# Two-layer hybrid trunk: the state-space outputs stand one position further behind their within-chunk kernels

## The chip, the cores and the metric

The kernel runs on 1 core of one Trainium2 chip. The metric is the device time of one execution in microseconds (us). Three executions of the kernel before took 2449.69, 2453.62 and 2454.12 us (median 2453.62). A fourth, with the profiler on, took 2454.61 us; its profile has a span of 2452.6 us from the first to the last instruction. All engine times below are from that one.

## The reference, cut to what matters

A batch of one, 256 tokens of width 2048, two layers. Each layer is a mixer with two branches side by side (stick-breaking attention, and an S5 diagonal state-space branch), merged by gates, then a channel mixer (dense SwiGLU in layer 0, top 2 of 8 experts in layer 1). The part that is touched is the state-space branch:

```python
def hybrid_mixer(h, w_in, ...):
    q, k, v, u, gate_a, gate_b = jnp.split(h @ w_in, cuts, axis=-1)
    o_attn = stick_breaking_attention(heads(q), heads(k), heads(v))
    y = jax.nn.gelu(s5_ssm(u, a_re, a_im, log_dt, b_re, b_im, c_re, c_im, d_skip))
    o_ssm = y * jax.nn.sigmoid(y @ w_glu)
    merged = (jax.nn.sigmoid(gate_a) * (o_attn @ p_attn)
              + jax.nn.sigmoid(gate_b) * (o_ssm @ p_ssm))
    return merged @ w_out

def s5_ssm(u, ...):                       # 64 groups of 16 channels, 64 complex states each
    ...
    _, _, x_re, x_im = lax.associative_scan(combine, (a_re_t, a_im_t, bu_re, bu_im), axis=1)
    y = einsum('bsgn,gpn->bsgp', x_re, c_re) - einsum('bsgn,gpn->bsgp', x_im, c_im) + d_skip * u
```

## The kernel before, in words

**The foreground.** Almost all the work is dense products of 256 token rows (two blocks of 128) with float32 weights. `chunk_mm` (L151) does 512 output columns at a time: it loads weights in tiles `wr` of two slices of 128 rows (512 KB) on the SP queue, splits each into a rounded part `wh` (ScalarE, L145) and a remainder `wl` (VectorE, L148), and issues three matmuls per slice and block (L166, L167, L168), each 128x512. Four slices make 24 matmuls; then it calls `pump()`. The pools `wr`, `wh` and `wl` have four buffers each, so the split runs at most four tiles, or 48 matmuls, ahead of TensorE.

**The background.** `pump()` advances Python generators, each by its rate, in steps that end at a `yield`. That decides where the small instructions of the attention heads and of the state-space branch stand between groups of 24 foreground matmuls, on every engine; after it, a scheduler may still shift single instructions. Each engine then works its own list in order: an instruction that waits holds everything behind it on that engine. The state-space generator runs at 1.05 steps per pump (`R_SSM`), and from the outputs on it is the only one left in the background, or nearly.

**The state-space branch.** The 256 steps are cut in 32 chunks of 8. For each of 8 blocks of 8 groups (index `gg`) `ssm_out` does:

- `products` (VectorE, L511 to L513, into the tile `PA`, with a ScalarE copy at L690): C times powers of A.
- `kern(gg)`: 8 matmuls (L635) give the response within a chunk; ScalarE copies it out of PSUM into `K2` (L639), VectorE adds the skip term (L642), the POOL queue writes it to a scratch in DRAM with 4 DMAs (L644, `kscr<-K`) and reads it back in Toeplitz form with one DMA of 512 KB (L651, `T<-kscr`). That read waits for the four writes.
- `outp(gg)`: 16 matmuls (L658 with `T`, L661 with `PA` and the chunk states `XS`), then a gelu on ScalarE (L665).
- `turn(gg)`: two transposes (L673) and a VectorE copy (L678). After the blocks 3 and 7 the POOL queue writes four blocks to DRAM (L681); both halves are read back as `yt` (L877) and copied on ScalarE (L880) where the gated output needs them.

A loop over `t` (L685) holds these in a software pipeline: in one turn of the loop `turn(t-3)`, the products of `t`, a yield, `outp(t-2)`, `kern(t-1)`, a yield. `outp` is held back until the attention is done. `PA`, `ptmp`, `K2`, `T` and `Y` all come from one pool of 28 slabs of 4 KB per partition, which the gates and the activations share: a slab can be written again only when its last reader is done.

The foreground around it is: the attention's output product (`oh` matmuls, 8 slices, 48 matmuls) and gate projections (`hh`, 16 slices, 96 matmuls), in turn.

Of the kernel before, what the change touches and what calls it, by code (L numbers as in the profile page):

```python
# [51 lines left out]
class Trunk:  # L52
# [558 lines left out]
    def ssm_out(self, l, U2, yscr):  # L611
        nc, i = self.nc, self.i
        V = nc.vector
        sp = self.sp

        dI = self.small([16, 16], tag="dI", bufs=1)
        self.tc.keep_in_program_order(nc.gpsimd.memset(dI, 0.0))
        for j in range(4):
            nc.gpsimd.dma_start(
                dI[j * 32 : j * 32 + 16],  # L620
                i["ssm_d"][l].rearrange("(a j) c -> j a c", j=4)[j].partition_broadcast(16))
        V.tensor_tensor(dI, dI, self.i16.unsqueeze(1).to_broadcast([P, 16, 16]), op=OP.mult)
        PA, T, Y = {}, {}, {}

        def wide(g):

            return sp["bA"][:, g : g + 2].rearrange("n g p -> n (g p)")

        def kern(gg):

            K2 = self.slab([8, 2, 16], name="K2")
            ps = self.paux()
            for gl in range(8):
                j, q = gl % 4, gl // 4
                nc.tensor.matmul(  # L635
                    ps[j * 32 : (j + 1) * 32, q * P : (q + 1) * P],
                    wide(gg * 8 + gl),
                    PA[gg][:, gl].rearrange("p t c -> p (t c)"), start=True, stop=True)
            nc.scalar.copy(  # L639
                K2.rearrange("p t q c -> p q t c"),  # L640
                ps[:, 0:256].rearrange("p (q t c) -> p q t c", q=2, t=8))
            V.tensor_tensor(K2[:, 0], K2[:, 0], dI[:, gg * 2 : gg * 2 + 2], op=OP.add)  # L642
            for j in range(4):
                nc.gpsimd.dma_start(  # L644
                    self.kscr[gg][:, 7:15, j * 32 : (j + 1) * 32],
                    K2[j * 32 : j * 32 + 16].rearrange("p t q c -> p t (q c)"))

            T[gg] = self.slab([8, 8, 16], name="T")
            ks = self.kscr[gg]
            win = bass.AP(ks.tensor, ks.offset, [[15 * P, 16], [P, 8], [1, 8 * P]])  # L650
            nc.gpsimd.dma_start(T[gg].rearrange("p t g c -> p (t g c)"), win)  # L651

        def outp(gg):
            ps = self.paux()
            for gl in range(8):
                j, q = gl % 4, gl // 4
                o = ps[j * 32 : (j + 1) * 32, q * P : (q + 1) * P]
                nc.tensor.matmul(  # L658
                    o.rearrange("c (t p) -> c t p", t=8), U2[gg // 4][:, gl, gg % 4], T[gg][:, :, j * 2 + q],
                    start=True, stop=False)  # L660
                nc.tensor.matmul(  # L661
                    o, self.XS[:, :, 0, gg * 8 + gl], PA[gg][:, gl].rearrange("p t c -> p (t c)"),
                    start=False, stop=True)
            yc = self.small([2, 16, 8], tag="sy", bufs=2)
            nc.scalar.activation(  # L665
                yc.rearrange("p q c t -> p q t c"),
                ps[:, 0:256].rearrange("p (q t c) -> p q t c", q=2, t=8), AF.Gelu_apprx_tanh)
            return yc

        def turn(gg, yc):  # L670
            ps = self.paux()
            for q in range(2):
                nc.tensor.transpose(  # L673
                    ps[:, q * P : (q + 1) * P], yc[:, q].rearrange("p c t -> p (c t)"), self.ident)
            h = gg // 4
            if gg % 4 == 0:
                Y[h] = self.slab([8, 4, 32], name="ysb")
            nc.vector.tensor_copy(Y[h][:, :, gg % 4], ps[:, 0:256].rearrange("p (g c) -> p g c", g=8))  # L678
            if gg % 4 == 3:

                nc.gpsimd.dma_start(  # L681
                    yscr[h].rearrange("(g q) j n -> (q j) g n", g=8), Y[h].rearrange("p g a c -> p g (a c)"))

        YC = {}
        for t in range(11):  # L685
            if t > 2:
                turn(t - 3, YC.pop(t - 3))
            if t < 8:
                PA[t] = self.slab([8, 8, 16], name="PA")
                nc.scalar.copy(PA[t][:, :, 0], sp["cA"][:, t * 8 : t * 8 + 8])  # L690

                self.products(t, PA[t][:, :, 1:8], sp["cA"], sp["cB"], 0, 7)
            yield
            if 2 <= t < 10:
                while not self.attn_done:
                    yield
                YC[t - 2] = outp(t - 2)
            if 1 <= t < 9:
                kern(t - 1)
            yield  # L700
# [610 lines left out]
```

## Time and profile before

| | |
|---|---|
| Median of three executions | 2453.62 us (2449.69 to 2454.12) |
| The profiled execution | 2454.61 us, span 2452.6 us |
| TensorE (PE) busy | 2395.9 us, 98% of the span |
| VectorE, ScalarE busy | 1630.7 us (66%), 1358.3 us (55%) |
| POOL busy | 100.6 us (4%) |
| State-space outputs, layer 0 and layer 1 | about 308 to 434 us and 1436 to 1556 us of the span |

PE is the TensorE matmul row, PEld its weight loads, DVE is VectorE, ACT is ScalarE, SP the queue that loads weights. A matmul's duration overlaps with the next one's, so the pace of PE is read from the starts of successive instructions and not from their durations. The profile puts a wait down to what released it.

### The profile page before, as it was taken

How to read it: one execution, taken by the hardware profiler on the slowest of the kernel's cores; microseconds unless marked ns; L12 is line 12 of the kernel's file. 1: busy time of each engine (PE TensorE's matmuls, PEld its weight loads, DVE VectorE, ACT ScalarE, POOL GpSimd, SP SyncE). 2: the span in 40 equal slices, each digit the busy share in tenths (PEclk: the TensorE clock that was granted, in tenths of full speed). 3: DMA queues.
4: the chain of work that ended last, by engine and by line, in shares of the span. 5: the costliest groups of instructions: out<-in, count | busy, mean ns of one | idle time of the engine just before them, and what ended most of it. 6: DMA issues, size and time to landing. Idle time of an engine off the chain costs nothing. (4 is left out here: it accounts for less than half of the span.)

```text
span 2452.6 us, 31712 instructions
## 1 busy us (share of the span) xinstructions
PE 2395.9 (98%) x11813; PEld 1959.6 (80%) x11813; DVE 1630.7 (66%) x1930; ACT 1358.3 (55%) x1676; POOL 100.6 (4%) x180
## 2 busy tenths in 40 slices
PE   9999988999999999999999999999999999999997
PEld 7878867888888888888888787788878888888875
DVE  7576954465545454454676866446558898988987
ACT  6455543544544444444546554454447777777775
POOL 0101011000000000000010011000000000000000
PEclk9999999999999999999999999999999999999998
DMA  7865466665556656566785556666549899898995
GB/s 262 227 193 172 151 197 178 214 215 184 185 192 187 190 190 187 190 205 199 224 275 157 155 172 208 196 194 208 175 143 362 309 346 360 294 357 312 367 360 192
DMA packets 297954, 556.99 MB, mean 227 GB/s; under 512 B 35552, under 2 KB 36896, under 8 KB 297792
## 3 DMA queue, kind: packets, MB, share of 16 engines
q1 hardware_dynamic: 284944, 517.52, 64.0%
q0 software_dynamic: 12848, 37.37, 5.1%
q8 instruction: 94, 1.54, 0.3%
q14 instruction: 68, 0.56, 0.1%
HBM read 543.86 MB, written 10.94 MB: 226 GB/s over the span
## 5 line engine op out<-in xcount | busy, mean ns | idle before, releaser
L148 DVE TENSOR_TENSOR wl<-wr,wh 128x1024 fp32r<-128x1024 f32 (+1 forms) x764 | 928.2, 1223 | 663.8 <-ACT wh L145 657.5
L145 ACT CAST wh<-wr 128x1024 fp32r<-128x1024 f32 (+1 forms) x764 | 801.6, 1053 | 851.3 <-PE pm L168 782.4
L166 PE MATMUL pm<-wh,hh 128*128 128x512 f32 x1536 | 605.6, 394 | 0.5 <-ACT hh L193 0.3
L167 PE MATMUL pm<-wl,hh 128*128 128x512 f32 x1536 | 600.9, 391 | 3.4 <-DVE wl L148 3.4
L168 PE MATMUL pm<-wh,hl 128*128 128x512 f32 x1536 | 600.5, 391 | 0.3 <-DVE hl L194 0.3
L167 PEld LDWEIGHTS pm<-wl,hh 128*128 128x128 f32 x1536 | 289.2, 188 | 64.1 <-DVE wl L148 6.2
L166 PEld LDWEIGHTS pm<-wh,hh 128*128 128x128 f32 x1536 | 289.0, 188 | 61.9 <-issue 1.2
L168 PEld LDWEIGHTS pm<-wh,hl 128*128 128x128 f32 x1536 | 289.1, 188 | 60.8 <-DVE hl L194 0.9
L148 DVE TENSOR_TENSOR wl<-ring,wh 128x1024 fp32r<-128x1024 f32 x214 | 254.9, 1221 | 22.3 <-ACT wh L145 15.9
L145 ACT CAST wh<-ring 128x1024 fp32r<-128x1024 f32 x214 | 221.7, 1053 | 50.6 <-PE pm L168 47.8
L167 PE MATMUL pm<-wl,eh 128*128 128x512 f32 x512 | 202.3, 395 | 1.3 <-DVE wl L148 0.8
L166 PE MATMUL pm<-wh,eh 128*128 128x512 f32 x512 | 200.5, 392 | 1.4 <-ACT wh L145 1.4
L168 PE MATMUL pm<-wh,el 128*128 128x512 f32 x512 | 201.1, 393 | 0.0
L167 PE MATMUL pm<-wl,ah 128*128 128x512 f32 x512 | 200.2, 391 | 0.2 <-DVE wl L148 0.2
L168 PE MATMUL pm<-wh,al 128*128 128x512 f32 x512 | 199.9, 390 | 0.0
L166 PE MATMUL pm<-wh,ah 128*128 128x512 f32 x512 | 199.7, 390 | 0.0
L167 PEld LDWEIGHTS pm<-wl,eh 128*128 128x128 f32 x512 | 96.5, 188 | 28.6 <-DVE wl L148 8.8
L166 PEld LDWEIGHTS pm<-wh,eh 128*128 128x128 f32 x512 | 96.5, 188 | 21.5 <-ACT wh L145 1.5
L167 PEld LDWEIGHTS pm<-wl,ah 128*128 128x128 f32 x512 | 96.2, 188 | 21.2 <-DVE wl L148 1.5
L166 PEld LDWEIGHTS pm<-wh,ah 128*128 128x128 f32 x512 | 96.2, 188 | 19.8
L168 PEld LDWEIGHTS pm<-wh,el 128*128 128x128 f32 x512 | 96.6, 189 | 19.2
L168 PEld LDWEIGHTS pm<-wh,al 128*128 128x128 f32 x512 | 96.2, 188 | 19.6
(310 smaller groups left out, 2566.9 us busy)
## 6 DMA issues: line engine op xcount, KB each, us to landing
wr<-in_w_in_dram SPq DMA_DIRECT2D x254, 512.0 KB, 3.9
ring<-in_moe_w_up_dram SPq DMA_DIRECT2D x72, 512.0 KB, 5.8
ring<-in_moe_w_gate_dram SPq DMA_DIRECT2D x71, 512.0 KB, 5.9
ring<-in_moe_w_down_dram SPq DMA_DIRECT2D x71, 512.0 KB, 5.9
wr<-in_w_out_dram SPq DMA_DIRECT2D x64, 512.0 KB, 3.8
wr<-in_ffn_w_gate_dram SPq DMA_DIRECT2D x64, 512.0 KB, 4.2
wr<-in_ffn_w_up_dram SPq DMA_DIRECT2D x64, 512.0 KB, 3.5
wr<-in_ffn_w_down_dram SPq DMA_DIRECT2D x64, 512.0 KB, 3.9
```

The lines of the kernel that those rows point to most:

```text
L145: t = self.nc.scalar.copy(h, raw)
L148: self.nc.vector.tensor_tensor(l, raw, h, op=OP.subtract)
L166: nc.tensor.matmul(ps[b], XH(k, b), h, start=st, stop=False)
L167: nc.tensor.matmul(ps[b], XH(k, b), l, start=False, stop=False)
L168: nc.tensor.matmul(ps[b], XL(k, b), h, start=False, stop=sp)
```

## The change

The loop over `t` has one turn more (12 for 11); `outp` and `turn` move one turn later, `kern` and the products stay. So one more `T` and one more `PA` are alive at a time, and the last output and its transposes stand later in the foreground.

```diff
-        for t in range(11):
-            if t > 2:
-                turn(t - 3, YC.pop(t - 3))
+        for t in range(12):
+            if t > 3:
+                turn(t - 4, YC.pop(t - 4))
             if t < 8:
                 PA[t] = self.slab([8, 8, 16], name="PA")
...
             yield
-            if 2 <= t < 10:
+            if 3 <= t < 11:
                 while not self.attn_done:
                     yield
-                YC[t - 2] = outp(t - 2)
+                YC[t - 3] = outp(t - 3)
             if 1 <= t < 9:
                 kern(t - 1)
```

On TensorE, layer 0, the end of the first attention output product. Before, the last two of the 16 matmuls of `outp(0)` stand here, and `kern(1)` and the gate projection follow (`pa` is a PSUM tile of the background, `pm` of the foreground):

```order
L658 MATMUL pa_2990<-T_2905,U_97_502 32x128
L661 MATMUL pa_2990<-PA_2769,XS_1108 32x128
L635 MATMUL pa_3010<-PA_2847,bA_957 32x128 x8
L166 MATMUL pm_3030<-wh_3034,hh_116 128x512
L167 MATMUL pm_3030<-wl_3035,hh_116 128x512
L168 MATMUL pm_3030<-wh_3034,hl_120 128x512
```

Now only `kern(1)` stands at that place:

```order
L167 MATMUL pm_2911<-wl_2963,oh_1998 128x512
L168 MATMUL pm_2911<-wh_2962,ol_1999 128x512
L635 MATMUL pa_2991<-PA_2847,bA_957 32x128 x8
L166 MATMUL pm_3011<-wh_3015,hh_116 128x512
L167 MATMUL pm_3011<-wl_3016,hh_116 128x512
L168 MATMUL pm_3011<-wh_3015,hl_120 128x512
```

and `outp(0)`, with the same `T_2905`, comes 48 foreground matmuls later, ahead of `kern(2)`:

```order
L658 MATMUL pa_3091<-T_2905,U_97_502 32x128
L661 MATMUL pa_3091<-PA_2769,XS_1108 32x128
L635 MATMUL pa_3111<-PA_2948,bA_957 32x128 x8
L166 MATMUL pm_3011<-wh_3130,hh_118 128x512
L167 MATMUL pm_3011<-wl_3131,hh_118 128x512
```

Counted over both layers, 40 to 48 foreground matmuls stood between a `kern(gg)` and its `outp(gg)` (72 for the first of layer 1); now 96 stand there, and 72 in four cases: blocks 2 and 3 of layer 0, blocks 6 and 7 of layer 1. The last `turn` stands 48 foreground matmuls later in layer 0 and 24 in layer 1. The numbers of instructions are the same on every engine.

On ScalarE, the copy into `PA` for block 6 of layer 0, with the semaphores that each instruction waits for (DMASW are the POOL queue's DMAs, DMAHW the weight loads). Before:

```order
L639 COPY K_676_3341<-pa_3342 128x2x8x16 [waits DMASW5_49,DMASW6_49,DMASW0_49,DMASW7_49,DVE_49,PE_49]
L145 CAST wh_3492<-wr_3490 128x1024 [waits DMAHW6_49,PE_49]
L145 CAST wh_3538<-wr_3536 128x1024 [waits DMAHW7_49,DVE_49,PE_49]
L690 COPY PA_3400<-cA_2705 128x8x16
L145 CAST wh_3544<-wr_3542 128x1024 [waits DMAHW0_49,DVE_49,PE_49]
```

Now:

```order
L639 COPY K_673_3318<-pa_3319 128x2x8x16 [waits PE_49]
L856 ACTIVATE ga_3258<-ga_3258 128x1024 [waits Activation_49]
L145 CAST wh_3462<-wr_3460 128x1024 [waits DMAHW5_49,DVE_49,PE_49]
L145 CAST wh_3468<-wr_3466 128x1024 [waits DMAHW6_49,DVE_49,PE_49]
L690 COPY PA_3376<-cA_2705 128x8x16 [waits DMASW4_49,DMASW3_49,DMASW5_49,DMASW2_49,DVE_49]
L145 CAST wh_3514<-wr_3512 128x1024 [waits DMAHW7_49,PE_49]
L145 CAST wh_3520<-wr_3518 128x1024 [waits DMAHW0_49,PE_49]
```

With more slabs alive, the slab of this `PA` is the one that `K2` has just left: the copy waits for the four DMAs that write `K_673` to DRAM, and the casts of weights stand behind it. Five of the 16 `PA` copies wait so now (two of layer 0, three of layer 1) that did not before.

## Rows read from the trace of the kernel before

**Rows 1.** The page: busy us, share of the span and instructions of each engine.
```profile
PE 2395.9 (98%) x11813; PEld 1959.6 (80%) x11813; DVE 1630.7 (66%) x1930; ACT 1358.3 (55%) x1676; POOL 100.6 (4%) x180
```
**Rows 2.** Waits of PE: waiting line, releaser, us in total, times, longest.
```profile
PE pa L658 <- DMA T<-kscr: 25.7, 12, 4.9
PE pm L167 <- DVE wl L148: 4.3, 7, 1.8
```
**Rows 3.** Stretches: length, busy us (instructions) by engine, PEclk, DMA share, GB/s.
```profile
308.00:434.00 126.00, 110.40 (x795) 88.44 (x794) 67.72 (x74) 51.61 (x65) 23.16 (x44) 0.96 0.62 185
434.00:1436.00 1002.00, 999.72 (x4685) 822.89 (x4684) 577.83 (x684) 483.84 (x606) 25.51 (x42) 1.00 0.62 196
1436.00:1556.00 120.00, 109.50 (x791) 88.58 (x790) 67.51 (x73) 54.88 (x68) 21.62 (x41) 0.97 0.62 187
```
**Rows 4.** PE in order of time: start, duration, instruction, [idle before, releaser].
```profile
308.31 0.65 PE L635 MATMUL pa<-PA,bA 128*32 128x128 f32 x16
...
317.89 0.39 PE L166 MATMUL pm<-wh,oh 128*128 128x512 f32 x1
...
319.71 0.39 PE L168 MATMUL pm<-wh,ol 128*128 128x512 f32 x1
324.17 0.45 PE L658 MATMUL pa<-T,U 128*32 128x128 f32 x8 [4.08 <-DMA T<-kscr]
...
1519.51 0.46 PE L658 MATMUL pa<-T,U 128*32 128x128 f32 x8 [0.67 <-DMA T<-kscr]
...
1520.39 0.69 PE L635 MATMUL pa<-PA,bA 128*32 128x128 f32 x16
1521.02 0.50 PE L166 MATMUL pm<-wh,hh 128*128 128x512 f32 x1
...
1535.80 0.68 PE L658 MATMUL pa<-T,U 128*32 128x128 f32 x8 [4.95 <-DMA T<-kscr]
```
**Rows 5.** Stretches behind the four longest of these waits; columns as above.
```profile
324.10:328.50 4.40, 4.33 (x54) 3.53 (x55) 1.33 (x2) 1.01 (x2) 1.27 (x3) 0.61 0.06 18
382.00:386.20 4.20, 4.20 (x54) 3.33 (x53) 0.19 (x1) 1.83 (x3) 1.52 (x3) 0.63 0.25 92
411.00:414.00 3.00, 2.92 (x49) 2.53 (x50) 0.00 (x0) 0.68 (x2) 0.00 (x0) 0.54 0.56 187
1535.70:1541.40 5.70, 5.60 (x58) 4.69 (x59) 0.19 (x1) 1.20 (x3) 1.83 (x4) 0.61 0.07 21
```
**Rows 6.** POOL in order of time, block 0 of layer 0.
```profile
312.63 2.09 POOL L644 DMA_DIRECT2D kscr<-K  x4 [97.85 <-DVE K L642]
318.23 0.53 POOL L651 DMA_DIRECT2D T<-kscr  x1 [3.51 <-DMA kscr<-K]
```
**Rows 7.** Tile T: instruction times in ns (min/median/max), and DMA landing.
```profile
L651 POOL DMA_DIRECT2D T<-kscr x16: 533/536/547, 318.2 to 1543.4; - x16
...
DMA to landing us min/median/max: 4.2/5.9/7.5
```
**Rows 8.** Tile K: the same.
```profile
L644 POOL DMA_DIRECT2D kscr<-K x64: 528/531/542, 312.6 to 1541.1; - x64
...
DMA to landing us min/median/max: 1.7/2.9/6.4
```
**Rows 9.** Groups by line: busy us, mean ns of one, idle before.
```profile
L148 DVE TENSOR_TENSOR wl<-wr,wh 128x1024 fp32r<-128x1024 f32 (+1 forms) x764 | 928.2, 1223 | 663.8 <-ACT wh L145 657.5
L145 ACT CAST wh<-wr 128x1024 fp32r<-128x1024 f32 (+1 forms) x764 | 801.6, 1053 | 851.3 <-PE pm L168 782.4 <-DMA wr<-in_w_in_dram 38.9 <-issue 16.9
L511 DVE TENSOR_TENSOR PA<-cA,AT 128x896 f32<-128x896 f32 x16 | 17.3, 1083 | 0.0
```
**Rows 10.** Tiles yscr and yt in layer 0: POOL's writes and reads, ACT's copies.
```profile
L681 POOL DMA_DIRECT2D yscr<-ysb x2: 909/910/912, 372.5 to 433.0; - x2
L877 POOL DMA_DIRECT2D yt<-yscr x2: 554/561/568, 433.9 to 437.9; - x2
L880 ACT COPY yf<-yt x2: 2079/2083/2087, 468.6 to 474.1; 128x1024 f32<-128x1024 f32 x2
...
DMA to landing us min/median/max: 4.7/4.8/4.8
```

## The prediction

> **What bounds the kernel now.** I read the busy shares first: PE is busy for 98% of the span, the next engine for 66% [rows 1]. What PE doesn't do while others work is therefore lost time, and what others wait for costs nothing. Next the waits of PE: by far the largest is L658, the first matmul of `outp`, which waits for the DMA that reads `T`: 25.7 us in 12 of 16 cases, at most 4.9 us; the second is 4.3 us [rows 2]. Then the busy times by stretch: in the 1002 us between the two state-space stretches PE is busy for 999.7 us at a granted clock of 1.00; in the two stretches for 110.4 of 126 us and 109.5 of 120 us, at 0.96 and 0.97 [rows 3]. So these 246 us have two losses: the waits, and a lower clock. The order of PE in time shows the first and the stretches behind the long waits the second: after a wait of 4.08 us PE runs at 0.61 for some 4 us, and so behind the one of 4.95 us and two more [rows 4, 5]; a clock of 0.61 is a mixture of the two levels, 1.2 and 2.4 GHz.
>
> Why `T` is late: block 0 of layer 0 starts `kern` at 308.31 us, POOL issues the four writes at 312.63 and the read at 318.23 when the writes have landed, and PE goes on at 324.17 [rows 4, 6]. The chain takes 15.9 us. Block 6 of layer 1 takes 15.4 us (1520.39 to 1535.80) [rows 4]. In that time PE has 40 to 48 foreground matmuls to do. Eight of them take 1.82 us (317.89 to 319.71), so 0.2275 us each and 10.9 us for 48 [rows 4].
>
> **What the change removes.** With 96 foreground matmuls between `kern` and its `outp` the cover is 21.8 us, plus the `outp` and `kern` of neighbouring blocks that stand between (1519.51 to 1521.02, 1.5 us) [rows 4]. In the four cases with 72 it is 16.4 + 1.5 = 17.9 us, and 17.3 us for the last block of layer 1, which has only an `outp` between (0.9 us). The longest chain of the trace that ended in a wait, 15.9 us, is below each of these. All 12 waits should go: 25.7 us.
>
> The lower clock goes with them, since it stands behind the four longest of them. What it costs is the missing share of the clock times the stretch [rows 5]: 0.39 x 4.4 = 1.72, 0.37 x 4.2 = 1.55, 0.46 x 3.0 = 1.38, 0.39 x 5.7 = 2.22; sum 6.9 us. As a check: 0.04 x 126 + 0.03 x 120 = 8.6 us by the whole stretches, which holds the time at low clock inside the waits as well [rows 3]. I take 6.9.
>
> **What it adds and moves.** No instruction is added. `turn` and `outp` move as they are, with their ACT and DVE copies, and cost PE the same at any place. Three things need cover:
>
> - The last `turn`, with the POOL write and the reads of `yt` behind it, comes 48 foreground matmuls (10.9 us) later in layer 0 and 24 (5.5 us) in layer 1. In layer 0 the second `yt` was issued at 437.9 and landed 4.8 us later, at 442.7; ACT copies the first at 468.6 [rows 10]. 25.9 us of spare become 15: nothing. In layer 1 more foreground work lies between.
> - On POOL the write of the first half of y changes places with writes and reads of `kscr` near it. It holds the queue for 0.91 us [rows 10], in a chain with at least 1.4 us (17.3 less 15.9) to spare: nothing.
> - Five `PA` copies on ACT (and the product on DVE that writes the same tile) now wait for the four writes of a `K2`, with casts of weights queued behind, which PE needs. For block 6 of layer 0: `kern` to the first write 4.3 us, 1.6 us to the fourth [rows 4, 6], landing 2.9 us at the median and 6.4 at most [rows 8], so the copy starts 8.8 to 12.3 us after `kern`. The tile cast next is wanted 72 foreground matmuls, 17.9 us, after `kern`; between lie a product of 1.1 us and a subtraction of 1.2 us on DVE [rows 9]. It is ready at 11.1 to 14.6 us: hidden, with 3.3 us left at worst. Without that cover it would cost each of the five what it is late by.
>
> No row shows these new waits themselves; the bounds are 0 and, with every landing at its maximum, still 0. I see no gain either beyond the two terms, as PE has no other wait in these stretches worth a microsecond.
>
> **The sum.** 25.7 + 6.9 = 32.6 us. The profiled execution took 2454.61 us: 2422.0. It lies 1.0 us above the median of the three, so I predict 2421 us against 2453.62, 1.3% faster.
>
> **The rivals.**
>
> - *The chain grows and part of the waits stays.* PE will work through the same transfers in some 32 us less, so the DMA engines, busy for 0.62 of the stretches, come to 0.62 x 246 / 213 = 0.72. If every write lands at 6.4 us and every `T` at 7.5 us [rows 7, 8], the chain is 4.3 + 1.6 + 6.4 + 7.5 = 19.8 us, over the cover in the four cases by 1.9, 1.9, 1.9 and 2.5 us: 8 us come back, 2429. For it: landings scatter, 4.2 to 7.5 us. Against it: these maxima were never met in one chain.
> - *The clock doesn't come back.* Then only the waits go: 2453.6 - 25.7 = 2428. Against it: 1002 us at 1.00 with PE as dense as it would be here [rows 3].
> - *POOL's issues are stretched by a denser VectorE.* DVE's busy share in the stretches rises from 0.55 (135 of 246 us) to about 0.63 [rows 3]. If each of the five issues of a chain were held for one subtraction, 1.22 us [rows 9], the chain would be 15.9 + 6.1 = 22.0 us; the four short cases would wait some 4.3 us each, 17 us, and two or three of them lose clock: about 2441. Against it: none of 80 issues took longer than 0.547 us, with DVE busy more than half the time [rows 7, 8]. The Trainium skill (SBUF — State Buffer, section "SBUF: two separate sides") has a rule that speaks for this rival: a DMA issued from GpSimd has its descriptors written by that engine, which a VectorE copy in a two-port mode locks out, so that a DMA of about 0.62 us takes about 3.1 us. An estimate from that page would be five times 2.5 us, 12.4 us on the chain, instead of 6.1. The durations of the trace do not agree with it here.
> - *Slower: VectorE and ScalarE come late with weights.* The five `PA` copies hold ACT and DVE; if the `K2` writes land later than 17.9 - 4.3 - 1.6 - 1.1 - 1.2 = 9.7 us, PE waits for `wl` instead of for `T`. To lose the 32.6 us again, five cases must each be late by 6.5 us, a landing of 16 us; beyond that the kernel is slower, at 18 us by 10 us: 2464. For it: PE does wait for `wl` now and then, 7 times, 4.3 us [rows 2], and ACT and DVE are the engines that feed it. Against it: the longest of 64 landings is 6.4 us [rows 8].
>
> **How the numbers follow.** The forecast 0.84, with a range of its own of 2416 to 2426 (the spread of the three executions is 4.4 us, and the clock's term could be 2 us more or less); the grown chain 0.07; the clock 0.04; POOL 0.02; late weights 0.03. The range 2414 to 2433 holds the first three. A difference of under 0.2%, 4.9 us, can't be told from none here. Faster by more: 0.95, as all but the last rival and accidents lead there; the same 0.03; slower 0.02.
>
> **What would show it.** Right: L658 is gone from the waits of PE, or has under 2 us; both stretches have PEclk 0.99 or 1.00 and are together about 32 us shorter; new rows of ACT (L690) and DVE (L511) waiting for `kscr<-K`, a few us, with `wl` at PE no longer than the 4.3 us of before. Wrong: L658 with waits at blocks 2 and 3 of layer 0 and 6 and 7 of layer 1 (the chain grew); PEclk still 0.96 to 0.97 without waits (the clock); POOL issues of a microsecond and more; or L166 and L167 waiting for `wh` and `wl` in the two stretches by as much as L658 did, which would make the prediction wrong as a whole.

## The result

The changed kernel takes 2421.26 us in the median of four runs (2419.84 to 2425.37), the kernel before 2451.72 us beside it (2449.69 to 2454.12). The ratio is 0.9884, with a 95% interval of 0.9868 to 0.9899: by the ratio 28 us less (25 to 32); the two medians differ by 30.5. A second series of six runs gave 2423.1 us against 2453.32, ratio 0.9879 (0.9859 to 0.9898). 2421 was predicted.

The profiled execution of the changed kernel took 2425.37 us with a span of 2423.5 us. Its waits of PE (line, releaser, us in total, times, longest), first three rows:

```profile
PE pm L167 <- DVE wl L148: 4.2, 6, 2.2
PE pa L708 <- DVE t L733: 2.4, 2, 1.9
PE pa L182 <- DMA x<-in_x_dram: 2.1, 1, 2.1
```

The row of 25.7 us that led this list in [rows 2] is gone, and the wait for `wl` has not grown (4.2 for 4.3 us). The same stretches as in [rows 3] (length, busy us of PE, PEld, DVE, ACT, POOL with instructions, PEclk, which is the granted clock of TensorE as a share of full speed, DMA share, GB/s):

```profile
308.00:434.00 126.00, 125.45 (x881) 101.18 (x880) 76.32 (x82) 62.81 (x75) 24.13 (x45) 1.00 0.73 221
434.00:1436.00 1002.00, 999.83 (x4707) 823.00 (x4706) 581.25 (x689) 482.18 (x608) 29.40 (x49) 1.00 0.62 196
1436.00:1556.00 120.00, 119.48 (x830) 97.03 (x829) 71.25 (x76) 61.42 (x72) 18.67 (x34) 1.00 0.72 220
```

PE is busy for 125.45 of 126 us where it was for 110.40, at a clock of 1.00 for 0.96 and 0.97. The DMA share rises from 0.62 to 0.73 and 0.72: the same transfers in less time. The distance between `kern` and its `outp`, which [rows 4] show as 15.9 and 15.4 us with the wait in it, is now without a wait; block 2 of layer 0, one of the four with 72 foreground matmuls (PE in order of time):

```profile
336.01 0.63 PE L635 MATMUL pa<-PA,bA 128*32 128x128 f32 x16
...
355.93 0.45 PE L658 MATMUL pa<-T,U 128*32 128x128 f32 x8
```

The chain behind it is much as it was in [rows 7, 8]; tiles T and K (times of an issue in ns, landings in us, minimum, median and maximum):

```profile
L651 POOL DMA_DIRECT2D T<-kscr x16: 533/533/544, 320.8 to 1511.6; - x16
...
DMA to landing us min/median/max: 4.3/5.8/8.1
```
```profile
L644 POOL DMA_DIRECT2D kscr<-K x64: 528/528/542, 315.6 to 1508.5; - x64
...
  ACT PA L690: 0.9, 2
  DVE PA L511: 0.2, 1
...
DMA to landing us min/median/max: 1.7/3.0/4.6
```

The last list also names who waited for these writes: the new waits of the `PA` copy and product are there, 0.9 us in two cases and 0.2 us in one. PE's wait for `wl` did not grow by them. In the stretch of each layer PE has one wait left, of 0.5 us, for a gelu result at a `turn`.

To see where the time went, take one line that both profiles have behind each stretch, L899 (transposes of the gated output; first and last start). Before:

```profile
L899 PE MATMUL pa<-consts,sg x16: 270/272/329, 497.6 to 515.6; 128*128 128x128 f32 x16
...
L899 PE MATMUL pa<-consts,sg x16: 270/272/329, 1659.0 to 1677.0; 128*128 128x128 f32 x16
```

After, with the first `kern` ahead of it:

```profile
311.60 0.65 PE L635 MATMUL pa<-PA,bA 128*32 128x128 f32 x16
```
```profile
L899 PE MATMUL pa<-consts,sg x16: 270/273/329, 481.5 to 499.5; 128*128 128x128 f32 x16
...
L899 PE MATMUL pa<-consts,sg x16: 270/273/330, 1629.2 to 1647.1; 128*128 128x128 f32 x16
```

From the first `kern` (308.31 before) to L899 of layer 0 it was 189.3 us and is 169.9: 19.4 less. From there to L899 of layer 1, 1161.4 and 1147.7: 13.7 less. Together 33.1 us, where 32.6 was forecast. The two spans differ by only 29.1 us because this execution came to the first `kern` 3.3 us later (2.1 us of it is the opening's wait for `x` in the first list) and took 0.7 us longer from the start of the last L899 group to its end (794.3 for 793.6). The change touches neither.

### The profile page after: what moved, and what is told of

It reads as the page before. It is cut to its first block, busy times and chain, and to the rows that moved or that the text cites. A ratio compares the mean times of both kernels' runs of the same rounds, so it can differ in the third digit from the quotient of the medians.

```text
span 2423.5 us, 31710 instructions
## 1 busy us (share of the span) xinstructions
PE 2389.9 (99%) x11813; PEld 1955.9 (81%) x11813; DVE 1630.0 (67%) x1930; ACT 1359.6 (56%) x1676; POOL 100.4 (4%) x180
## 5 line engine op out<-in xcount | busy, mean ns | idle before, releaser
L148 DVE TENSOR_TENSOR wl<-ring,wh 128x1024 fp32r<-128x1024 f32 x214 | 255.0, 1222 | 22.2 <-ACT wh L145 15.9
L168 PEld LDWEIGHTS pm<-wh,el 128*128 128x128 f32 x512 | 96.6, 189 | 19.2
```

Source lines behind the costliest of these rows:

```text
L148: self.nc.vector.tensor_tensor(l, raw, h, op=OP.subtract)
L168: nc.tensor.matmul(ps[b], XL(k, b), h, start=False, stop=sp)
```

## The experiments

The theory: `T` arriving late held PE, the low clock stood behind the longest of these waits, and nothing else counts. The rivals: the order itself gains (a longer pipeline, other places on ScalarE and VectorE); the low clock has a cause of its own.

**Half of the change: `turn` later, `outp` not.**

```diff
-        for t in range(11):
-            if t > 2:
-                turn(t - 3, YC.pop(t - 3))
+        for t in range(12):
+            if t > 3:
+                turn(t - 4, YC.pop(t - 4))
```

> Half of the change alone: the loop has 12 turns and the transposes (turn) come one position later, but outp stays one position behind its kern. If the gain is T arriving in time, nothing changes: 40 to 48 foreground matmuls stand between kern and outp as before, L658 waits for T some 26 us (20 to 32) and the time is that of before, 2448 to 2455 us. If the gain came from one more turn of the pipeline, from the later transposes or from the later writes of y, the time falls towards 2421 us.

Measured: 2448.21 us in the median of ten executions, one of which took 3191.82 us; ratio 0.9983 (0.9967 to 0.9999). The wait stays:

```profile
PE pa L658 <- DMA T<-kscr: 22.3, 13, 4.2
```

The 4 us less go with shorter waits in the profiled execution: in layer 1 none was over 2.4 us, and the clock there stayed at 1.00. Whether the moved `turn` shortened them or chance did is not shown. The 30 us do not come from one more turn of the loop.

**The wait taken away in the order of before.** `T` is read from an input matrix, ahead of `kern`'s matmuls; the writes of `K2` stay, their read-back goes.

```diff
+            T[gg] = self.slab([8, 8, 16], name="T")
+            win = i["w_glu"][l][gg * P : (gg + 1) * P]
+            nc.gpsimd.dma_start(T[gg].rearrange("p t g c -> p (t g c)"), win)
             K2 = self.slab([8, 2, 16], name="K2")
...
-            T[gg] = self.slab([8, 8, 16], name="T")
-            ks = self.kscr[gg]
-            win = bass.AP(ks.tensor, ks.offset, [[15 * P, 16], [P, 8], [1, 8 * P]])
-            nc.gpsimd.dma_start(T[gg].rearrange("p t g c -> p (t g c)"), win)
```

> The order of before, but T no longer depends on kern: it is read from an input matrix (512 KB, so the output is not the reference's) and its DMA is issued ahead of kern's own steps; the writes of K2 stay. If the waits for T and the clock behind them are all that the change removed, this order without the change reaches the changed kernel: no wait at L658, granted clock 0.99 to 1.00 in both stretches, 2419 to 2424 us. If the distance or the order itself matters (ScalarE's and VectorE's places, slabs), it stays above 2430. If the low clock comes from the short 32-column matmuls and not from the waits, the waits go and the clock stays at 0.96 and 0.97: about 2427.

Measured: 2422.12 us, ratio 0.9875 (0.9853 to 0.9897), no wait at `outp`:

```profile
308.00:434.00 126.00, 125.42 (x882) 101.44 (x881) 75.23 (x81) 63.64 (x76) 23.90 (x44) 1.00 0.71 225
...
1436.00:1556.00 120.00, 120.00 (x806) 97.77 (x805) 71.56 (x77) 58.08 (x69) 21.06 (x38) 1.00 0.69 217
```

The old distance without the dependence (in two blocks, 3 of layer 0 and 6 of layer 1, only 24 foreground matmuls stood between) reaches the changed kernel. So the order as such is worth nothing that these runs can tell; and the short 32-column matmuls, which all still run, don't lower the clock.

**Half a position.** `outp(t - 3)` stands ahead of the products of `t`, not behind the yield.

> outp half a position later than before: 72 foreground matmuls between kern and outp in 12 blocks, and 48 in four (blocks 2 and 3 of layer 0, 6 and 7 of layer 1, where the rate gives a double step). Theory: 72 matmuls and what stands between are 17 to 18 us, more than any chain seen (16 us), so the 12 wait for nothing; the four with 48 (11 us) wait 1 to 5 us each, 4 to 12 us in all, with one or two stretches of low clock: 2424 to 2433 us. Rival: T needs the full position, because the chain grows when PE doesn't wait: waits in most blocks, 2435 us and more. Rival: half a position is as good, 2421.

Measured: 2426.25 us, ratio 0.9893 (0.9874 to 0.9912), PEclk 1.00, and

```profile
PE pa L658 <- DMA T<-kscr: 1.3, 2, 0.7
```

The twelve blocks with 72 matmuls wait for nothing, as worked out. The four with 48 were expected to wait 4 to 12 us and waited 1.3: there I had left out that `kern`'s own matmuls and the neighbours' `outp`, `kern` and `turn` stand between here too. The distance was 14.1 to 15.0 us in them, not 11, and eight of the twelve chains that ended in a wait before were shorter than 14.1 us. Half a position takes nearly all of the gain.

**Yet one position further.** In the changed loop, 13 turns, `outp(t - 4)` and `turn(t - 5)`.

> outp yet one position later than in the change, 120 to 144 foreground matmuls behind kern in most blocks, and one more T and PA alive. There is no wait left to remove: the theory says no further gain, 2418 to 2424 us. Rival: each position further gains some: 2410 and less. Rival: the slabs run short, ScalarE and VectorE wait for the writes of K2 and PE for wl: 2427 us and more, with L167's wait for wl well over 5 us.

Measured: 2426.17 us, ratio 0.989 (0.9871 to 0.9909), beside 2423.1 for the changed kernel in the same series. No further gain, and 2 us above the range expected by the theory. The 3 us more than the changed kernel are under the 0.2% that the prediction set as the least that can be told; the expected `wl` wait of over 5 us did not come (4.6), but small waits did, of PE for the gelu's result and for the products:

```profile
PE pa L673 <- ACT sy L665: 1.9, 1, 1.9
...
PE pa L635 <- DVE K L642: 0.7, 1, 0.7
...
PE pa L635 <- DVE PA L513: 0.5, 2, 0.2
```

**The changed kernel again.** 

> The changed kernel again, on the same chip as the three runs beside it: 2419 to 2425 us, no wait at L658, PEclk 1.00 in both stretches. The half position was 5 us slower than the first runs of the changed kernel with only 1.3 us of waits; if those 5 us are a difference between chips, this run shows its counterpart.

Measured: 2423.1 us, no wait at L658, PEclk 1.00 in both stretches. It lies between the first series and the half position, so of the 5 us that seemed to separate those two some 2 can lie between series.

**A longer chain in the changed kernel.** `T` is read twice.

```diff
-            nc.gpsimd.dma_start(T[gg].rearrange("p t g c -> p (t g c)"), win)
+            for _ in range(2):
+                nc.gpsimd.dma_start(T[gg].rearrange("p t g c -> p (t g c)"), win)
```

> The changed kernel, with T read twice, the second read behind the first. The chain gets longer by one issue and one landing, some 6 us: 18 to 22 us instead of 12 to 16. If the cover is what was worked out (23 us with 96 foreground matmuls, 17 to 18 with 72), the twelve blocks with 96 wait for nothing or less than 1 us and the four with 72 wait 1 to 5 us each, 4 to 16 us in all, with up to two stretches of low clock: 2426 to 2441 us, and L658's waits stand at blocks 2 and 3 of layer 0 and 6 and 7 of layer 1. If the margin is larger than worked out, 2421; if smaller, waits in most blocks and 2450 and more.

Measured: 2444.42 us, ratio 0.9966 (0.9954 to 0.9977), outside what was expected. PE's wait is back, and in eight blocks, not four:

```profile
PE pa L659 <- DMA T<-kscr: 17.5, 8, 6.0
```

The chains that ended in a wait were 23.6 to 28.6 us, where 18 to 22 were expected. They grew by more than one read, since POOL works its list in order: the second read waits on the queue until the first has landed, and the next block's writes stand behind it. On VectorE the second block's `K2` was ready at 321.4 us (321.26 + 0.18):

```profile
321.26 0.18 DVE L642 TENSOR_TENSOR K<-K,dI 128x32 f32<-128x32 f32 x1
```
```profile
318.05 0.54 POOL L652 DMA_DIRECT2D T<-kscr  x1 [3.72 <-DMA kscr<-K]
323.64 0.53 POOL L652 DMA_DIRECT2D T<-kscr  x1 [5.06 <-DMA T<-kscr]
324.17 2.13 POOL L644 DMA_DIRECT2D kscr<-K  x4
```

but POOL wrote it only at 324.17, after the second read of block 0. So the cover holds for a chain whose queue is free; when the queue is held each block hands its lateness to the next. The 17.5 us of waits and some 6.8 us at low clock (the missing share of the clock, summed over pieces of 2 us, as in all such sums below) make 24.3 us, for the 21.3 us by which its median lies above the changed kernel beside it and 16.8 between the two profiled executions (2440.69 and 2423.88). The sum is too large by 3 to 7.5 us. Of that, 2.6 us are low clock inside the waits, which it counts twice; and far from the branch the profiled execution of the changed kernel lost some 6 us more to the low clock than this one (7.7 and 1.7 us, over pieces of 10 us).

**The clock, first try: small matmuls ahead of four long waits.**

```diff
+            if gg in ((0, 4, 6), (6,))[l]:
+                for _ in range(40):
+                    self.tc.keep_in_program_order(nc.tensor.matmul(
+                        ps[:, 256:384], self.identb, self.maskb, start=True, stop=True, skip_group_check=True))
```

> The kernel before with 40 matmuls of 128x128 in bfloat16 (0.055 us each, 2.2 us) ahead of outp in the four blocks that had the long waits (0, 4 and 6 of layer 0, 6 of layer 1). They write a part of a PSUM tile that nothing reads. They take the place of waiting and add nothing as long as the wait is longer than 2.2 us. If the low clock is PE's answer to standing idle, it stays high behind the shorter waits: up to 6.9 us less than before, 2443 to 2449 us, and PEclk of both stretches 0.98 to 1.00, with the end of each wait where it was. If the low clock has another cause (the short matmuls of outp and kern, power), the clock stays at 0.96 and 0.97 and the time at 2452 or a little more.

Measured: 2452.56 us, ratio 0.9994 (0.9982 to 1.0005), PEclk 0.97 in both stretches. The filler took the place of waiting (18.1 us are left of 25.7), but the clock still fell behind a wait of 1.98 us (`kern` takes 1.11 us for 0.65), and not behind one of 3.44 us elsewhere in the same run:

```profile
319.85 2.41 PE L657 MATMUL pa<-maskb,identb 128*128 128x128 bf16 x40
324.23 0.45 PE L662 MATMUL pa<-T,U 128*32 128x128 f32 x8 [1.98 <-DMA T<-kscr]
...
325.15 1.11 PE L635 MATMUL pa<-PA,bA 128*32 128x128 f32 x16
...
368.22 0.45 PE L662 MATMUL pa<-T,U 128*32 128x128 f32 x8 [3.44 <-DMA T<-kscr]
...
369.12 0.66 PE L635 MATMUL pa<-PA,bA 128*32 128x128 f32 x16
```

**The clock, second try: the foreground's kind of matmul.** As above, with 10 matmuls of 128x512 on tiles of `hh`.

> As the run with the 40 small matmuls, in the same four blocks of the order of before, but the filler is 10 matmuls of the foreground's own kind (128x512, 2.3 us), written to the PSUM tile before outp starts it anew. If the clock falls because PE stands without such work, waits shortened to under some 2.5 us leave it at 1.00 in both stretches and the 6.9 us of the clock come back: 2444 to 2448 us, with the waits for T plus the filler still some 26 us. If it falls whatever stands ahead of the wait, as behind the small matmuls, PEclk stays at 0.96 to 0.97 and the time at 2450 to 2454.

Measured: 2449.7 us, ratio 0.9983 (0.9968 to 0.9997); waits 12.0 us in 8 cases, and the filler 9.2. The time lies between the two expected ranges. The clock fell less often (some 5.1 us lost by it in the two stretches, for 8.5 before), but it did fall, behind 2.05, 2.17 and 2.51 us. One of them, us by us:

```profile
325.07 0.45 PE L663 MATMUL pa<-T,U 128*32 128x128 f32 x8 [2.05 <-DMA T<-kscr]
```
```profile
325.00:326.00 1.00, 0.93 (x32) 0.94 (x36) 0.00 (x0) 0.00 (x0) 0.00 (x0) 1.00 0.80 158
326.00:327.00 1.00, 1.00 (x25) 0.73 (x18) 0.00 (x0) 0.64 (x1) 0.00 (x0) 0.50 0.84 324
327.00:328.00 1.00, 1.00 (x6) 0.79 (x3) 0.19 (x1) 0.37 (x2) 0.00 (x0) 0.50 0.26 90
328.00:329.00 1.00, 1.00 (x4) 0.71 (x4) 0.00 (x0) 0.00 (x0) 0.89 (x2) 0.50 0.00 0
329.00:330.00 1.00, 1.00 (x5) 0.82 (x4) 0.00 (x0) 0.00 (x0) 1.00 (x3) 0.80 0.16 33
```

Here the low level, 1.2 GHz, comes about a microsecond after PE goes on, while it works, and costs 0.5 + 0.5 + 0.5 + 0.2 = 1.7 us. It is not always so late: before, in the wait of 4.95 us that ended at 1535.80, it came while PE still stood:

```profile
1533.00:1534.00 1.00, 0.00 (x0) 0.00 (x0) 0.00 (x0) 0.00 (x0) 0.00 (x0) 0.67 0.99 252
1534.00:1535.00 1.00, 0.00 (x0) 0.00 (x0) 0.00 (x0) 0.00 (x0) 0.00 (x0) 0.50 0.99 236
```

Both tries leave what sets it off open.

**The clock, third try: only the long waits, only the others.** As in the run with the free `T`, for five blocks in one kernel and for the eleven others in the other (there the line ends in `== False`):

```diff
+            free = (gg in ((0, 3, 4, 6), (6,))[l]) == True
```

> The order of before; T is read from an input matrix ahead of kern's steps (so the output is not the reference's) only in the five blocks that had the longest waits: 0, 3, 4 and 6 of layer 0 and 6 of layer 1. In the profile of before they waited 4.08 + 2.64 + 3.01 + 3.70 + 4.95 = 18.4 us, and the low clock stood behind four of them. If the clock's cost belongs to the long waits, 18.4 + 6.9 = 25.3 us go: about 2427 us (2423 to 2431), PEclk 1.00 in both stretches, some 7 us of waits left in the other blocks. If the clock falls just as often behind the waits that are left, or the waits move to other blocks, 2434 and more.

> The complement: T is free in the eleven other blocks (their output is not the reference's) and depends on kern in those five. If only the long waits carry the low clock, 7.3 us go and the clock stays: about 2446 us (2441 to 2449), PEclk 0.96 to 0.98, with 18 us of waits left in the five blocks. If any wait counts for the clock, it gets better here too: 2440 and less.

Measured: 2433.09 us (ratio 0.9918, 0.9902 to 0.9934) and 2448.55 us (0.9979, 0.9968 to 0.999), beside 2454.25. The waits that are left, and the first stretch, of the one:

```profile
PE pa L664 <- DMA T<-kscr: 10.7, 9, 2.3
```
```profile
308.00:434.00 126.00, 120.47 (x849) 97.20 (x841) 71.96 (x78) 60.09 (x73) 23.80 (x44) 0.99 0.68 211
```

and of the other:

```profile
PE pa L664 <- DMA T<-kscr: 19.2, 5, 5.2
```
```profile
308.00:434.00 126.00, 109.42 (x786) 88.07 (x785) 65.99 (x72) 51.70 (x65) 22.34 (x42) 0.95 0.61 185
```

Without the long waits there is one low stretch left (1.7 us); with only the long ones the low stretches cost 8.5 us, as before. The first kernel came out some 2 us above its expected range: the other blocks waited 10.7 us, not 7, as their chains are not the same in each execution. Waits and clock together account for it: 25.7 - 10.7 = 15.0 us of waits and 8.5 - 1.7 = 6.8 of clock are 21.8, and 21.2 were measured between the medians, 23.4 between the two profiled executions (the low clock again holds some of the waiting). By the waits alone it would have been 15. The second saved 25.7 - 19.2 = 6.5 us of waits and no clock, and measured 5.7.

## Why the prediction was right

**The bound and the cover.** `outp` waited for `T`, and the distance decides. It held on both sides: no wait in the changed kernel, the same time without the dependence, the wait back with a longer chain. The chains that ended in a wait were 11.3 to 17.0 us in the runs with the old distance; the changed kernel has 19.4 to 25.6 us between. The cover was worked out too small, on the safe side (17.3 to 17.9 us with 72 foreground matmuls, measured 19.4 to 20.0): `kern`'s own matmuls and the `turn` of other blocks stand between too, and the sum left them out. From `kern` to the issue of `T` the changed kernel took 6.7 to 9.2 us; with its longest landing, 8.1 us, that is 17.3 at most.

**The sum.** Waits 25.7 and clock 6.9 us, 32.6 forecast; between the marks above 33.1 us went, in layer 0 19.4 (15.2 of waits and 4.65 of clock by the forecast) and in layer 1 13.7 (10.5 and 2.2). Layer 1 gained 1 us more than the two terms, and a place that the prediction did not look at accounts for it: ahead of the branch PE waits for VectorE (tile `t`), and the clock fell there before but not in the changed kernel's execution, though the wait was as long. Before and after:

```profile
1406.65 1.72 PE L708 MATMUL pa<-t,consts 128*128 128x384 f32 x4 [1.86 <-DVE t L733]
1407.00:1408.00 1.00, 1.00 (x4) 0.61 (x3) 1.00 (x2) 0.00 (x0) 0.00 (x0) 0.53 0.08 16
```
```profile
1390.29 1.13 PE L708 MATMUL pa<-t,consts 128*128 128x384 f32 x4 [1.90 <-DVE t L733]
1391.00:1392.00 1.00, 1.00 (x9) 0.90 (x8) 1.00 (x3) 0.49 (x1) 0.00 (x0) 1.00 0.06 16
```

That is 1.7 us of the 13.7, and no run shows that the change has a part in it: this wait is 1.85 to 1.92 us in the profiles of all twelve kernels of this document, and the clock fell with it in eight of them, also in the run with the free `T`, which is as fast as the changed kernel. The medians differ by 30.5 and 30.2 us: the profiled execution of before, 2454.61 us, took longer than each of the four timed beside the changed kernel; with the same distance the half change waited 22.3 us, so the waits differ by some us from one execution to the next. The forecast of the median to within 1 us is thus part luck: the error of 2 us in the gain and the difference of 2 us between two medians of the same kernel before (2453.62 and 2451.72) cancelled.

**The clock's term** had the right size (the pieces of 2 us give 8.5 us in the two stretches, of which 1.6 lie inside waits), but "it goes with them" rested on more than the trace of before had. The runs with and without the long waits show that it goes; the two fillers, and the wait for `t`, show that it is not decided by the length of the wait alone.

**The moved steps** cost next to nothing, as forecast. Two of the five `PA` copies waited, 0.9 us in all, on writes with a longest landing of 4.6 us, far from the 9.7 us from which PE would have noticed.

**The rivals.** The chain did not grow in the way that counts: the share of the DMA engines came to 0.72 and 0.73, the 0.72 that was worked out, and the landings stayed at 5.8 and 3.0 us in the median (the longest of `T` was 8.1 us for 7.5). POOL's issues did not stretch (at most 0.544 us). Late weights did not come. What no rival had is the queue: the run with two reads shows that POOL's order makes lateness pass from block to block, so that the margin in the changed kernel, 3 to 10 us per block, no longer holds when one block keeps the queue about as long as the blocks are apart, some 12 to 13 us. In that run the first four blocks kept it for 11.8 to 15.8 us each, from the first write to the end of the second read.

No version here beats the changed kernel; the run without the dependence, 2422.12 us, says that this wait has nothing left to give that can be told here.

## What to carry to other kernels

When an engine that bounds the kernel waits for a round trip through a queue and DRAM, add up the chain from the trace and set it against the work that stands between in the new order, in the same units; place the reader where the least cover exceeds the longest chain, and no further. To check that the wait is the whole cause, take away the dependence and keep the order: the time that this gives is about what a rearrangement can reach that does no more than remove this wait. Count a held queue as part of the chain of whatever stands behind it.

## What the runs showed of the hardware

The granted clock fell to 1.2 GHz up to some 1 us after PE had gone on, in long waits while it still stood, and each fall cost 1.7 us, or 3.4 us where it stayed low for longer (as behind the wait of 4.95 us). It fell behind waits of 4.08, 3.01, 3.70 and 4.95 us, and with a filler just ahead also behind 1.98, 2.05, 2.17 and 2.51 us; it did not behind 2.64 us in the kernel before nor behind 3.44 us in the run with the small filler. With one and the same wait, 1.85 to 1.92 us for the tile `t`, it fell in eight of the twelve profiles and not in the other four. The length of a wait alone does not tell whether the clock falls, and work put just ahead of the wait, short or of full size, did not prevent it.
